# An encoder layer on one core: the last norm's shift is written to the output rows ahead of time, and finished rows are added to it by their stores

## The chip, the cores and the metric

The kernel runs on one core of one Trainium2 chip. The metric is the device time of one execution in microseconds, the median of several runs. PE is the matrix engine, DVE the vector engine, ACT the scalar engine, POOL the GpSimd engine; SP only issues DMAs.

## The reference

One encoder layer (DEPTH is 1) on x of 1024 positions by 1024 channels, in float32: a Fourier token mixer, then a gated MLP with a three-tap convolution over positions, each with a modulated norm ahead of it and a norm behind it. The part that matters here is the end:

```
h = modulate(x, sh2, sc2)
y = conv_gated_ffn(h, *ffn_p[i])                              # F = 2816
x = layer_norm(ALPHA * x + g2[:, None, :] * y, *ln_ffn[i])    # y * g + b per channel
return x
```

The last norm takes mean and variance over the 1024 channels of each position, scales to unit variance, multiplies by a gain per channel (`ffn_g`) and adds a shift per channel (`ffn_b`). Both are given to the kernel as 128 equal rows.

## The kernel before, in words

The work comes in stages: the adaLN vectors and the Fourier mixer (to about 300 us), the up projection with convolution and gate (to about 640 us), the down projection, and the last norm. Matmul operands are split in a high and a low part (ACT copies the high part, DVE or POOL subtracts for the low part, line 54) and each product is three matmuls (`hl3`, lines 284 to 286).

The up projection runs over 22 columns `j` of 128 features. `up_load(j)` issues two loads of 512 KB on SP for each column, and the gated result of each column is stored to `gd` in HBM by a DMA on POOL.

The down projection is a seven-product Strassen scheme over 512 x 512 halves, run in the order of products `(1, 2, 5, 6, 3, 7, 4)`, each over six pairs `i` of blocks; `(p, i)` names a step. `C[half][m]` holds 128 output rows by 1024 channels: half 0 is the upper 512 rows (called u0 to u3 here), half 1 the lower 512 rows (r0 to r3). The upper rows are complete ahead of product 4; `upper_half`, `upper` and `normed` finish them during products 7 and 4: square and sum on ACT (line 877), the power of -0.5 on POOL (line 426, a helper), the small product `nb` on DVE (line 880), the scaling on ACT (line 881), the gain (line 882) and the shift (line 883) on DVE, then `store`, on POOL for the upper half. The lower rows wait for product 4: `lower(m)` prepares them, and `evac(4, m, ...)` multiplies by the gate (line 821 for m of 0 to 2, line 833 in quarters for m of 3), adds (822, 834), takes the variance (827 to 829, or `bn_stats` on lines 835 to 839 for m of 3), takes the power on POOL (830, 840), and then runs two DVE passes over the whole row, line 852 for mean and gain and line 853 for scale and shift, then `store`, on SP for the lower half.

The order of the work on DVE, ACT and PE is chosen by a planner when the kernel is built. From the down projection on, SP and POOL are taken out of that and keep the order in which the program writes their instructions:

```
ctx.enter_context(tc.manual_schedule(engines={mybir.EngineType.SP, mybir.EngineType.Pool}))
```

`ffg` and `ffb` (gain and shift) are loaded on SP at step (7, 1), lines 945 and 947. `E(name)` gives POOL for the names in a fixed list and DVE for the rest; those of the last norm are all DVE.

Of the kernel before, what the change touches and what calls it, by code (L numbers as in the profile page):

```python
# [8 lines left out]
F32 = mybir.dt.float32  # L9
F32R = mybir.dt.float32r  # L10
AF = mybir.ActivationFunctionType
ALU = mybir.AluOpType
# [3 lines left out]
D = 1024  # L16
# [20 lines left out]
def encoder_layer(ctx: ExitStack, tc: tile.TileContext, I, out: bass.AP):  # L37
    nc = tc.nc
    act, dve, pool, pe, sp = nc.scalar, nc.vector, nc.gpsimd, nc.tensor, nc.sync

    cp = ctx.enter_context(tc.tile_pool(name="cp", bufs=1))
    sm = ctx.enter_context(tc.tile_pool(name="sm", bufs=6))
# [3 lines left out]
    def slot(i, shape, dt, name):  # L46
        return big.tile([128] + list(shape), dt, tag=f"s{i}", name=name)
# [8 lines left out]
    def E(name):  # L56
        return pool if name in ON_POOL else dve
# [152 lines left out]
    for t, t4 in pairs:  # L210
# [20 lines left out]
        rs = sm.tile([128, 2], F32, tag="rs2", name=f"rsa{t}")  # L231
# [9 lines left out]
    for c0 in (0, 512):  # L241
        cs = slice(c0, c0 + 512)
# [299 lines left out]
    sp.dma_start(cw, I["cw"])  # L542
    raws = {}

    def up_load(j):
        sl = (24, 27) if j == 0 else ((29, 30) if j % 2 else (27, 28))
        raws[j] = []
        for q in range(2):
            r = slot(sl[q], [4, 256], F32, f"wu{j}_{q}")
            sp.dma_start(r, I["w_up"][j, q])  # L550
            raws[j].append(r)

    up_load(0)
# [70 lines left out]
    A_slots = [33, 34, 35, 45, 46, 47, 48]  # L624
    for j in range(2, NB):
        up_load(j)
        raw = raws[j]
        A11, A21 = raw[0][:, :, 0:128], raw[0][:, :, 128:256]
        A12, A22 = raw[1][:, :, 0:128], raw[1][:, :, 128:256]
        S12 = slot(31, [2, 4, 128], F32, f"S12_{j}")  # L630
        S34 = slot(32, [2, 4, 128], F32, f"S34_{j}")
        S1, S2, S3, S4 = S12[:, 0], S12[:, 1], S34[:, 0], S34[:, 1]
        pool.tensor_tensor(S1, A21, A22, ALU.add)
        pool.tensor_tensor(S2, S1, A11, ALU.subtract)
        pool.tensor_tensor(S3, A11, A21, ALU.subtract)  # L635
        pool.tensor_tensor(S4, A12, S2, ALU.subtract)  # L636

        def product(n, a, tname):
            o = slot(A_slots[n], [2, 4, 128], F32R, f"a{j}_{n}")
            split(o[:, 0], o[:, 1], a)  # L640
            acc = xbank(f"x{j}_{n}")
            th, tl = ops[tname]
            for kt in range(4):
                hl3(acc, o[:, 0, kt, :], o[:, 1, kt, :], th[kt], tl[kt], kt == 0, kt == 3)
            return acc

        if j == NB - 1:
            g2 = slot(27, [D], F32, "g2")
            row_bcast(G2, g2, xbank)
        p12 = slot(6, [2, 512], F32, f"p12_{j}")  # L650
        u34 = slot(7, [2, 512], F32, f"u34_{j}")
        p1, u2, u3, u4 = p12[:, 0], p12[:, 1], u34[:, 0], u34[:, 1]
        uv_ = slot((2 * j) % 3, [S], F32, f"uv{j}")
        ug_ = slot((2 * j + 1) % 3, [S], F32, f"ug{j}")
        x = product(0, A11, "B11")
        act.activation(p1, x, AF.Copy)
        x = product(1, S2, "T2")
        dve.tensor_tensor(u2, x, p1, ALU.add)
        x5 = product(2, S1, "T1")
        dve.tensor_tensor(u4, x5, u2, ALU.add)  # L660
        x = product(3, A12, "B21")
        dve.tensor_tensor(uv_[:, 0:512], x, p1, ALU.add)
        x = product(4, S3, "T3")
        dve.tensor_tensor(u3, x, u2, ALU.add)
        dve.tensor_tensor(ug_[:, 512:], x5, u3, ALU.add)
        x = product(5, S4, "B22")
        dve.tensor_tensor(uv_[:, 512:], x, u4, ALU.add)
        x = product(6, A22, "T4")
        dve.tensor_tensor(ug_[:, 0:512], u3, x, ALU.subtract)
        gated(j, uv_, ug_)  # L670
# [120 lines left out]
        r0 = 512 * half + 128 * m  # L791
        sp.dma_start(xr[half, m], x1d[r0 : r0 + 128, :])

    def store(half, m):
        r0 = 512 * half + 128 * m
        (pool, sp)[half].dma_start(out[r0 : r0 + 128, :], C[half][m])

    def evac(p, m, x):
        c0, c1 = C[0][m], C[1][m]
        nm = f"f{p}{m}"  # L800
        if p == 1:
            act.activation(c1[:, L], x, AF.Copy, scale=-1.0)
        elif p == 2:
            dve.tensor_tensor(c0[:, L], c1[:, L], x, ALU.subtract)
        elif p == 5:
            act.activation(c1[:, R], x, AF.Copy)
        elif p == 6:
            dve.tensor_tensor(c1[:, L], x, c1[:, L], ALU.add)
            dve.tensor_tensor(c1[:, R], c1[:, R], c1[:, L], ALU.add)
        elif p == 3:  # L810
            dve.tensor_tensor(c0[:, R], c1[:, R], x, ALU.subtract)
        elif p == 7:
            dve.tensor_tensor(c1[:, R], c1[:, R], x, ALU.subtract)
            dve.tensor_tensor(c1[:, L], c1[:, L], x, ALU.subtract)
        else:
            st = st1[m]
            t = slot((33, 34)[m % 2], [512], F32, f"pg{m}")
            n = 512 // x_parts(m)
            rs = sm.tile([128, 1], F32, tag="rs", name=f"rs{nm}")
            if m in sq_rows:  # L820
                dve.tensor_tensor(t, x[0], g2[:, L], ALU.mult)
                dve.scalar_tensor_tensor(c1[:, L], t, -1.0, c1[:, L], ALU.mult, ALU.add, accum_out=st[:, 0:1])
                nmu = sm.tile([128, 1], F32, tag="nmu", name=f"nmu{nm}")
                dve.tensor_scalar(nmu, st[:, 0:1], st[:, 1:2], -1.0 / D, ALU.add, ALU.mult)
                ss = sm.tile([128, 1], F32, tag="ss", name=f"ss{nm}")
                junk = cp.tile([128, D], mybir.dt.bfloat16, tag="sel", name=f"junk{nm}")
                act.activation(junk, c1, AF.Square, bias=nmu, accum_out=ss)
                ve = sm.tile([128, 1], F32, tag="ve", name=f"ve{nm}")
                dve.tensor_scalar(ve, ss, 1.0 / D, EPS, ALU.mult, ALU.add)
                pool.tensor_tensor(rs, ve, mhalf, ALU.pow)  # L830
            else:
                for k in range(0, 512, n):
                    dve.tensor_tensor(t[:, k : k + n], x[k // n], g2[:, k : k + n], ALU.mult)
                    dve.tensor_tensor(c1[:, k : k + n], c1[:, k : k + n], t[:, k : k + n], ALU.subtract)
                    dve.bn_stats(st[:, k // n, :], c1[:, k : k + n])
                mv = sm.tile([128, 2], F32, tag="mv", name=f"mv{nm}")
                dve.bn_aggr(mv, st)
                ve = sm.tile([128, 1], F32, tag="ve", name=f"ve{nm}")
                dve.tensor_scalar(ve, mv[:, 1:2], EPS, None, ALU.add)
                pool.tensor_tensor(rs, ve, mhalf, ALU.pow)  # L840
                nmu = sm.tile([128, 1], F32, tag="nmu", name=f"nmu{nm}")
                dve.tensor_scalar(nmu, mv[:, 0:1], -1.0, None, ALU.mult)
            nd = D
            lo, hi = slice(0, nd), slice(nd, D)
            if nd < D:
                nb = sm.tile([128, 1], F32, tag="nb", name=f"nb{nm}")
                E(f"nbt{m}").tensor_tensor(nb, nmu, rs, ALU.mult)
                act.activation(c1[:, hi], c1[:, hi], AF.Identity, scale=rs, bias=nb)
                E(f"ng{m}").tensor_tensor(c1[:, hi], c1[:, hi], ffg[:, hi], ALU.mult)
                E(f"nf{m}").tensor_tensor(c1[:, hi], c1[:, hi], ffb[:, hi], ALU.add)  # L850
            if nd:
                dve.scalar_tensor_tensor(c1[:, lo], c1[:, lo], nmu, ffg[:, lo], ALU.add, ALU.mult)
                dve.scalar_tensor_tensor(c1[:, lo], c1[:, lo], rs, ffb[:, lo], ALU.mult, ALU.add)  # L853
            store(1, m)

    sq_rows = (0, 1, 2)

# [15 lines left out]
    def normed(half, m, nmu):  # L873
        c, nm = C[half][m], f"fn{half}{m}"
        ss = sm.tile([128, 1], F32, tag="ss", name=f"ss{nm}")
        junk = cp.tile([128, D], mybir.dt.bfloat16, tag="sel", name=f"junk{nm}")
        act.activation(junk, c, AF.Square, bias=nmu, accum_out=ss)
        rs = inv_std(ss, nm)
        nb = sm.tile([128, 1], F32, tag="nb", name=f"nb{nm}")
        E(f"unb{m}").tensor_tensor(nb, nmu, rs, ALU.mult)  # L880
        act.activation(c, c, AF.Identity, scale=rs, bias=nb)
        E(f"ug{m}").tensor_tensor(c, c, ffg, ALU.mult)
        E(f"ub{m}").tensor_tensor(c, c, ffb, ALU.add)  # L883
        store(half, m)

    st1 = []
# [28 lines left out]
    for n, (p, i) in enumerate(steps):  # L915
# [27 lines left out]
        if (p, i) == (7, 1):  # L943
            ffg = slot(25, [D], F32, "ffg")
            sp.dma_start(ffg, I["ffn_g"])
            ffb = slot(26, [D], F32, "ffb")
            sp.dma_start(ffb, I["ffn_b"])
        if p == 4 and 0 <= i - 1 < 4:
            lower(i - 1)
        while split_n < min(len(steps), n + 2):  # L950
# [128 lines left out]
```

## Time and profile before

| | |
|---|---|
| runs, median | 871.85 us (869.87 to 873.02, 3 runs) |
| profiled execution, time | 872.16 us |
| profiled execution, span | 870.4 us |
| granted PE clock, mean | 0.974 |
| PE busy | 798.9 us (92%) |
| DVE busy | 720.4 us (83%) |
| ACT busy | 387.8 us (45%) |
| POOL busy | 312.9 us (36%) |
| DMA moved | 131.02 MB, mean 151 GB/s |

The span runs from the first to the last event of the profiled execution; the time has some 1.8 us around it. Busy shares are averages over all stages, so the rows of one stretch say more than this table. In rows of a timeline the columns are the start in us from the span's start, the duration in us, the engine, the line, the operation and its output and inputs. A bracket at the end says how long the engine was idle before, and what released it. An instruction's duration on DVE and ACT takes in some pipeline time, so that the next one can start a little before it ends.

### The profile page before, as it was taken

To read this page: it belongs to the slowest core of one execution; us is meant where nothing else is said; L and a number is where in the kernel's file an instruction comes from. 1 tells how busy PE (TensorE), PEld (TensorE's weight loads), DVE (VectorE), ACT (ScalarE), POOL (GpSimd) and SP (SyncE) were. 2 spreads that over 40 slices of the span, in tenths; PEclk is the share of its full clock that TensorE was granted. 3 is DMA by queue.
4 is the path that set the end of the run, shared out by engine and by line. 5 is a ranking of instruction groups with operands and counts; after the bars stand their busy time and mean duration, and the time that the engine had idled before them with its cause. 6 is when DMAs were issued, how large, how long until landed. Compare 5 with 4: busy or idle time off the path is not lost.

```text
span 870.4 us, 10731 instructions
## 1 busy us (share of the span) xinstructions
PE 798.9 (92%) x3943; PEld 644.0 (74%) x3943; DVE 720.4 (83%) x991; ACT 387.8 (45%) x559; POOL 312.9 (36%) x244
## 2 busy tenths in 40 slices
PE   2699799998979999999999999999999989999990
PEld 1466577877858888888888888888878868887880
DVE  6972857899899999998888888888677795556998
ACT  7442514577454344444444444444454324335612
POOL 4776802498355444334343333431000122301102
PEclk9899899999989999999999999999999999999995
DMA  9658665572112212322212222210598886808703
GB/s 344 252 183 306 248 228 198 178 270 81 49 49 97 98 73 76 116 85 88 73 72 73 98 97 81 89 49 25 186 375 296 279 213 113 157 25 270 261 27 143
DMA packets 49749, 131.02 MB, mean 151 GB/s; under 512 B 5512, under 2 KB 6664, under 8 KB 49696
## 3 DMA queue, kind: packets, MB, share of 16 engines
q1 hardware_dynamic: 41008, 106.47, 34.6%
q0 software_dynamic: 8400, 22.81, 9.8%
q10 hardware_dynamic: 288, 1.05, 0.3%
q8 instruction: 31, 0.51, 0.2%
q14 instruction: 22, 0.18, 0.1%
HBM read 110.39 MB, written 19.92 MB: 150 GB/s over the span
## 4 chain that ended last, share of the span: by engine, by line
PE 54%; DVE 8%; DMA 7%; issue 3%; POOL 1%; SPq 0%; ACT 0%; DVEq 0%; POOLq 0%
PE x L286 14%; PE x L284 14%; PE x L285 14%; PE o L285 4%; PE o L286 4%; PE o L284 4%; DMA gr<-gd 2%; DMA xu<-x1d 2%; DVE d_1l L54 2%; DMA wd<-in_w_down_dram 1%; DVE d_0l L54 1%; DMA wd_2r<-in_w_down_dram 1%; DMA Sg<-gd 1%; DVE C L853 1%; DVE C L883 1%
## 5 line engine op out<-in xcount | busy, mean ns | idle before, releaser
L284 PE MATMUL x<-Hh,a 128*128 128x512 f32 (+2 forms) x416 | 155.8, 378 | 5.3 <-ACT a L53 5.3
L285 PE MATMUL x<-Hl,a 128*128 128x512 f32 (+2 forms) x416 | 156.6, 377 | 3.9 <-DVE Hl L54 3.1
L286 PE MATMUL x<-Hh,a 128*128 128x512 f32 (+2 forms) x416 | 155.8, 375 | 0.0
L285 PE MATMUL o<-d_1l,d_0h 128*128 128x512 f32 (+1 forms) x299 | 115.0, 385 | 6.5 <-DVE d_1l L54 4.3
L286 PE MATMUL o<-d_1h,d_0l 128*128 128x512 f32 (+1 forms) x299 | 114.7, 384 | 0.0
L284 PE MATMUL o<-d_1h,d_0h 128*128 128x512 f32 (+1 forms) x299 | 102.4, 382 | 0.0
L284 PEld LDWEIGHTS x<-Hh,a 128*128 128x128 f32 x416 | 78.7, 191 | 21.2 <-ACT a L53 6.0
L285 PEld LDWEIGHTS x<-Hl,a 128*128 128x128 f32 x416 | 79.0, 190 | 19.2 <-DVE Hl L54 4.4
L53 ACT ACTIVATE a<-S 128x512 fp32r<-128x512 f32 x80 | 50.4, 630 | 95.6 <-PE x L286 87.2
L286 PEld LDWEIGHTS x<-Hh,a 128*128 128x128 f32 x416 | 78.9, 190 | 14.5 <-issue 0.8
L588 POOL DMA_DIRECT2D gd<-ug x20 | 11.4, 569 | 170.2 <-DVE ug L587 170.2
L285 PEld LDWEIGHTS o<-d_1l,d_0h 128*128 128x128 f32 x299 | 56.6, 189 | 18.7 <-DVE d_1l L54 7.7
L54 DVE TENSOR_TENSOR a<-wu,a 128x512 fp32r<-128x512 f32 x60 | 63.6, 1060 | 3.0 <-ACT a L53 3.0
L286 PEld LDWEIGHTS o<-d_1h,d_0l 128*128 128x128 f32 x299 | 56.6, 189 | 10.8
L284 PEld LDWEIGHTS o<-d_1h,d_0h 128*128 128x128 f32 x299 | 56.3, 189 | 11.0
L54 DVE TENSOR_TENSOR a<-S,a 128x512 fp32r<-128x512 f32 x80 | 61.0, 763 | 0.8
L53 ACT ACTIVATE a<-wu 128x512 fp32r<-128x512 f32 x60 | 37.5, 625 | 40.1 <-PE x L286 38.2
L635 POOL TENSOR_TENSOR S<-wu 128x512 f32<-128x512 f32 x20 | 29.8, 1492 | 69.0 <-DVE a L54 60.3
L735 POOL DMA_DIRECT2D Sg<-gd x12 | 13.9, 1239 | 91.6 <-DVE d_0l L54 91.6
L579 DVE SCALAR_TENSOR_TENSOR t<-uv,cw,t 128x1023 f32<-128x1023 f32 x20 | 35.9, 1793 | 11.4 <-ACT t L578 11.3
L636 POOL TENSOR_TENSOR S<-wu,S 128x512 f32<-128x512 f32 x20 | 43.9, 2195 | 0.1
L53 ACT ACTIVATE d_0h<-Sg 128x1024 fp32r<-128x1024 f32 x15 | 15.9, 1062 | 58.1 <-PE o L285 58.1
(341 smaller groups left out, 1944.5 us busy)
## 6 DMA issues: line engine op xcount, KB each, us to landing
aw<-in_ada_w_dram SPq DMA_DIRECT2D x48, 512.0 KB, 6.2
wu<-in_w_up_dram SPq DMA_DIRECT2D x44, 512.0 KB, 3.2
gd<-ug POOLq DMA_DIRECT2D x20, 512.0 KB, 2.9
wd<-in_w_down_dram SPq DMA_DIRECT2D x20, 512.0 KB, 9.7
gr<-gd SPq DMA_DIRECT2D x15, 512.0 KB, 7.6
gA<-gd SPq DMA_DIRECT2D x10, 512.0 KB, 10.7
Sg<-gd POOLq DMA_DIRECT2D x10, 512.0 KB, 6.2
x<-in_x_dram SPq DMA_DIRECT2D x8, 512.0 KB, 6.1
```

Source lines behind the costliest of these rows:

```text
L53: act.activation(hi, src, AF.Copy)
L54: (eng or dve).tensor_tensor(lo, src, hi, ALU.subtract)
L284: pe.matmul(ps_ap, hi_l, hi_r, start=first, stop=False)
L285: pe.matmul(ps_ap, hi_l, lo_r, start=False, stop=False)
L286: pe.matmul(ps_ap, lo_l, hi_r, start=False, stop=last)
L579: dve.scalar_tensor_tensor(tt[:, 1:S], u[:, 0 : S - 1], w[:, 0:1], tt[:, 1:S], ALU.mult, ALU.add)
L588: pool.dma_start(gd[j], gg)
L635: pool.tensor_tensor(S3, A11, A21, ALU.subtract)
L636: pool.tensor_tensor(S4, A12, S2, ALU.subtract)
L735: pool.dma_start(raw_g[p, i] if p == 7 else Sg[i], gd[k0 : k0 + n, :, 512 * mh : 512 * mh + 512].rearrange("k p c -> p k c"), accum_op=ALU ...
L853: dve.scalar_tensor_tensor(c1[:, lo], c1[:, lo], rs, ffb[:, lo], ALU.mult, ALU.add)
L883: E(f"ub{m}").tensor_tensor(c, c, ffb, ALU.add)
```

## The change

During the up projection, each of the columns 4 to 11 issues one more DMA on SP: a copy of the 128 shift rows (`ffn_b`, 512 KB) from HBM straight to 128 rows of the output in HBM, placed behind that column's weight loads. After eight columns the whole output holds the shift. The later stores no longer overwrite: they add to what is there (`accum_op=ALU.add`), which DMAs issued from POOL can do, so all stores go out on POOL. The shift is no longer loaded to SBUF, and no engine adds it.

For the upper rows the DVE add of line 883 goes. For the lower rows, the two DVE passes of lines 852 and 853 become: a small product `nb` on DVE, the scaling on ACT, the product with the gain on DVE. The last row (m of 3) does scaling, product and store in two halves of 512 channels, the right half first.

```diff
+    up_load_ins = []
...
-            sp.dma_start(r, I["w_up"][j, q])
+            up_load_ins.append(sp.dma_start(r, I["w_up"][j, q]))
...
     for j in range(2, NB):
         up_load(j)
+
+        if 4 <= j < 12:
+            with tc.issue_after(up_load_ins[-1].ins):
+                sp.dma_start(out[128 * (j - 4) : 128 * (j - 3), :], I["ffn_b"])
...
-    def store(half, m):
+    def store(half, m, cs=slice(0, D)):
         r0 = 512 * half + 128 * m
-        (pool, sp)[half].dma_start(out[r0 : r0 + 128, :], C[half][m])
+        pool.dma_start(out[r0 : r0 + 128, cs], C[half][m][:, cs], accum_op=ALU.add)
...
-            nd = D
-            lo, hi = slice(0, nd), slice(nd, D)
...
-            if nd:
-                dve.scalar_tensor_tensor(c1[:, lo], c1[:, lo], nmu, ffg[:, lo], ALU.add, ALU.mult)
-                dve.scalar_tensor_tensor(c1[:, lo], c1[:, lo], rs, ffb[:, lo], ALU.mult, ALU.add)
-            store(1, m)
+            nb = sm.tile([128, 1], F32, tag="nb", name=f"nb{nm}")
+            dve.tensor_tensor(nb, nmu, rs, ALU.mult)
+            for hs in (R, L) if m == 3 else (slice(0, D),):
+                act.activation(c1[:, hs], c1[:, hs], AF.Identity, scale=rs, bias=nb)
+                dve.tensor_tensor(c1[:, hs], c1[:, hs], ffg[:, hs], ALU.mult)
+                store(1, m, hs)
...
-        E(f"ub{m}").tensor_tensor(c, c, ffb, ALU.add)
         store(half, m)
...
-            ffb = slot(26, [D], F32, "ffb")
-            sp.dma_start(ffb, I["ffn_b"])
```

`tc.issue_after(x)` only places the block's DMA behind `x` in SP's order; it waits for nothing.

More of the change, by code (lines that the diff above doesn't have):

```diff
@@ L842, in evac @@
                 dve.tensor_scalar(nmu, mv[:, 0:1], -1.0, None, ALU.mult)
-            nd = D
-            lo, hi = slice(0, nd), slice(nd, D)
[L845 to L850, printed above, removed]
-            if nd:
-                dve.scalar_tensor_tensor(c1[:, lo], c1[:, lo], nmu, ffg[:, lo], ALU.add, ALU.mult)
-                dve.scalar_tensor_tensor(c1[:, lo], c1[:, lo], rs, ffb[:, lo], ALU.mult, ALU.add)
-            store(1, m)
+            nb = sm.tile([128, 1], F32, tag="nb", name=f"nb{nm}")
[4 more added lines that the diff above has]
+                store(1, m, hs)
     sq_rows = (0, 1, 2)
```

## Prediction

> **What bounds the end now.** I read the busy time by stretch first, then the end of DVE, ACT and POOL in order of time, then the transfers.
>
> ```profile
> core 0: us, PE busy (x) PEld busy (x) DVE busy (x) ACT busy (x) POOL busy (x), PEclk, DMA share, GB/s
> 300.00:660.00 360.00, 359.54 (x1587) 297.46 (x1586) 315.18 (x391) 158.56 (x207) 113.78 (x83) 1.00 0.30 109
> ...
> 826.70:846.00 19.30, 19.30 (x107) 16.78 (x106) 19.30 (x35) 2.40 (x3) 0.56 (x1) 1.00 0.07 28
> 846.00:848.30 2.30, 2.23 (x19) 2.03 (x17) 2.30 (x4) 0.00 (x0) 0.88 (x2) 1.00 0.00 0
> 848.30:867.00 18.70, 0.00 (x0) 0.00 (x0) 17.99 (x35) 4.86 (x7) 5.00 (x6) 0.61 0.35 141
> ```
>
> PE is the bound through the up projection and still full to 848.3; then 18.7 us follow without a matmul, with DVE busy 17.99 of them. The change works on this end. Rows u0 to u3 below are the upper half of the output, r0 to r3 the lower half.
>
> ```profile
> 809.61 1.22 DVE L883 TENSOR_TENSOR C<-C,ffb 128x1024 f32<-128x1024 f32 x1
> 824.49 1.22 DVE L883 TENSOR_TENSOR C<-C,ffb 128x1024 f32<-128x1024 f32 x1
> 845.89 1.21 DVE L883 TENSOR_TENSOR C<-C,ffb 128x1024 f32<-128x1024 f32 x1
> 847.03 1.27 DVE L821 TENSOR_TENSOR pg<-o,g 128x512 f32<-128x512 f32 x2
> 848.88 0.67 DVE L822 SCALAR_TENSOR_TENSOR C<-pg,C 128x512 f32<-128x512 f32 x1
> 850.10 0.14 DVE L880 TENSOR_TENSOR nbfn<-nmufu,rs_fn 128x1 f32<-128x1 f32 x1
> 850.17 0.20 DVE L824 TENSOR_SCALAR nmuf<-stl 128x1 f32<-128x1 f32 x1
> 850.34 1.24 ACT L881 ACTIVATE C<-C,nbfn,rs_fn 128x1024 f32<-128x1024 f32 x1 [15.10 <-DVE nbfn L880]
> 851.48 1.13 ACT L827 ACTIVATE junkf<-C,nmuf 128x1024 bf16<-128x1024 f32 x1
> 852.52 0.19 ACT L827 ACTIVATION_READ_ACCUMULATOR junkf<-C,nmuf 128x1 f32 x1
> 852.62 1.21 DVE L882 TENSOR_TENSOR C<-C,ffg 128x1024 f32<-128x1024 f32 x1
> 854.21 0.13 DVE L829 TENSOR_SCALAR vef<-ssf 128x1 f32<-128x1 f32 x1
> 857.05 1.21 DVE L883 TENSOR_TENSOR C<-C,ffb 128x1024 f32<-128x1024 f32 x1
> 864.02 1.28 DVE L852 SCALAR_TENSOR_TENSOR C<-C,nmuf,ffg 128x1024 f32<-128x1024 f32 x1
> 865.40 1.28 DVE L853 SCALAR_TENSOR_TENSOR C<-C,rsf,ffb 128x1024 f32<-128x1024 f32 x1
> ```
>
> The reader sees DVE finishing u2 (845.89), closing r0 to r3 (from 847.03), finishing u3 in the holes (852.62, 857.05) and ending with the two full passes of each lower row. POOL matters as much:
>
> ```profile
> 822.16 0.14 DVE L424 TENSOR_SCALAR ve_fn<-ssfn 128x1 f32<-128x1 f32 x1
> ...
> 847.40 0.58 POOL L796 DMA_DIRECT2D out_dram<-C  x1 [20.14 <-DVE C L883]
> 848.00 0.57 POOL L426 TENSOR_TENSOR rs_fn<-ve_fn,mhalf 128x1 f32<-128x1 f32 x1
> 858.55 0.57 POOL L796 DMA_DIRECT2D out_dram<-C  x1 [9.98 <-DVE C L883]
> 859.14 2.85 POOL L830 TENSOR_TENSOR rsf<-vef,mhalf 128x1 f32<-128x1 f32 x3
> 861.97 1.34 POOL L840 TENSOR_TENSOR rsf<-vef,mhalf 128x1 f32<-128x1 f32 x1
> ...
> L796 SPq DMA_DIRECT2D out_dram<-C x4: 332/334/338, 861.6 to 866.7; - x4
> ...
> out_dram<-C SPq DMA_DIRECT2D x4, 512.0 KB, 2.6
> ```
>
> u3's power had its input at 822.3 and ran at 848.00, right behind u2's store; r0's had its input at 854.34 and ran at 859.14, right behind u3's store. So POOL keeps the written order, and a store that waits for its row holds every power behind it. The last store goes out on SP at 866.7 and lands 2.6 later, at 869.3; 1.1 more to the span's end, 870.4. The profiled execution took 872.16 around that span, the median shown is 871.85. I work on the span and put the difference onto the median.
>
> **The change, part by part.**
>
> Removed: four L883 adds. One holds DVE for 1.14 (845.89 to 847.03). Two of them (809.61, 824.49) lie in a stretch where DVE never pauses, so what follows comes 2.27 earlier; the third is the one before 847.03 itself. Together r0 could start at 847.03 - 3.4 = 843.6, but its product must be there:
>
> ```profile
> 844.29 0.40 PE L286 MATMUL o<-d_1h,d_0l 128*128 128x512 f32 x1
> ...
> 847.96 0.28 PE L286 MATMUL o<-d_1h,d_0l 128*128 128x256 f32 x1
> ```
>
> The first row is the last product of r0 (three 512-wide blocks close one after the other, then r3's 256-wide ones), ending 844.7; the second ends PE at 848.24. PE was full, so these stay. r0 starts at 844.9: 2.1 gained, not 3.4. If DVE is held up elsewhere the gain is zero.
>
> Moved: the lower rows' two DVE passes, L852 and L853 (1.28 each), become one ACT pass like L881 (1.24), one DVE product like L882 (1.21) and a tiny nb like L880 (0.14). DVE gets shorter by 4 x 1.2 us; ACT stood almost idle. But the stores go from SP to POOL, and there they stand between the powers: in written order POOL now has store u3, power r0, store r0, power r1, store r1, and so on. Where three powers ran together at 859.14, power r1 must now wait until r0 is scaled, multiplied and handed to its store. This is the price of the change: one closed round per row. Its steps, from the rows above: power 0.57; to DVE 0.2; nb 0.14; to ACT 0.1 (850.24 to 850.34); scaling 1.24; to DVE 0.05; product 1.21; to POOL 0.30 (847.10 to 847.40); store 0.58. That is 4.39 a row, 13.2 for three rows.
>
> Start of the first round: it needs store u3 gone and r0's variance. u2's product stays, its add goes, so store u2, power u3 and u3's nb all come some 5 us earlier (L882 of u3 then has the hole in which L883 of u2 stood, or one soon after). r0's variance: 844.9 + 3.07 (847.03 to 850.10: L821 and L822 of r0 and r1) + 0.2 (L824) + 1.33 (the square and its sum, 851.48 to 852.71, and a start) + 0.13 = 849.6 with nothing between. With u3's product between, 1.14 later, 850.8. I take 850.8, because L882 of u3 fell among these instructions before. Lower end 849.6.
>
> The last row is split in halves. Its power starts at 850.8 + 13.2 = 864.0, nb is through at 865.0. Halves of this size have rows:
>
> ```profile
> 833.15 0.62 ACT L53 ACTIVATE d_1h<-wd_10r 128x512 fp32r<-128x512 f32 x1
> 838.10 0.68 DVE L891 TENSOR_TENSOR C<-C,g 128x512 f32<-128x512 f32 x1
> ```
>
> 865.0 + 0.62 + 0.05 + 0.68 + 0.30 = 866.7 for the first half's store; 0.58 later, 867.3, the second's, whose product (ACT to 866.3, DVE to 867.0) is just done.
>
> The adding stores have no row of their own; these are nearest:
>
> ```profile
> q0 software_dynamic: 1389, 2.68, 101.2%
> ...
> L735 POOL DMA_DIRECT2D Sg<-gd x12: 1188/1197/1422, 684.3 to 745.0; - x12
> DMA to landing us min/median/max: 5.4/6.8/14.8
> ...
> out_dram<-C POOLq DMA_DIRECT2D x2, 512.0 KB, 2.9
> ```
>
> The first is the stretch 745 to 760, in which adding transfers alone filled all 16 engines: 2.68 MB in 15 us, 0.18 MB per us, so 1.4 us of data for a 256 KB half; a plain store of 512 KB took 2.9 in all. An adding transfer of 512 KB took at least 5.4, but with 1.2 of issue against 0.58 here. So the last half lands between 2.9 and 5.4 after its issue; I take 3.5, since half the bytes at half the speed resembles the plain whole row, plus some queueing behind the first half. 867.3 + 3.5 + 1.1 = 871.9. Against 870.4 that is 1.5 more: 871.85 + 1.5 = 873.35.
>
> The Trainium skill, "DMA: Bandwidth & Descriptors" (Anatomy of one DMA), puts a POOL-issued transfer at about 2.0 us plus its bytes over 436 GB/s. By it the last half would land in an estimated 2.6, and the sum would be 872.4; it holds for the plain store's 2.9, not for the 5.4 of the adding ones.
>
> Added: eight copies of 512 KB from HBM to HBM on SP, one behind each of eight weight loads.
>
> ```profile
> wu<-in_w_up_dram SPq DMA_DIRECT2D x44, 512.0 KB, 3.2
> ...
> 792.28 1.06 SPq L947 DMA_DIRECT2D ffb<-in_ffn_b_dram  x1
> ...
> DVE wd_0r L746 <- DMA wd_0r<-in_w_down_dram: 3.1, 1, 3.1
> ```
>
> A copy costs SP 0.33 and the queues between 1.3 and 2.8 us (plain store to adding speed). A weight pair lands 3.2 after its issue and has a column of about 360/22 = 16 us; DMA is 0.30 busy there. I cost them at nothing; without this cover, 8 x 2.8 = 22. The L947 load (512 KB, 1.06 of SP) goes from a crowded stretch, but the wait there, 3.1 for wd_0r, is for a load issued ahead of it: between 0 and 1 gained, I take 0. The adding stores of u0 to u2 double their transfer time in a stretch where DVE and PE read operands loaded long before: 0.
>
> **The rivals.**
>
> u3 holds the queue. If DVE's order leaves L882 of u3 where it is (852.62, less 2.1: 850.5), store u3 goes out at 852.0, power r0 at 852.6: 875.1. If it slides to where L883 stands (857.05 less 2.1 and 1.1), power r0 starts at 855.9: 878.4. For it: u2 and u3 were finished last in every hole, and power u3 waited 26 us. Against: its input comes 5 us earlier. It decides from a power r0 later than 852.0. About 876; chance 0.26.
>
> Row 0 first. If L821 and L822 of r0 run back to back, power r0 starts at 847.8, 3.0 earlier; with rounds of 4.07 (DVE and ACT free at once, as instructions follow each other at 1.14) another 1.0 goes: 869.3, and with the plain landing 2.9, 868.7. For it: DVE has room. Against: before, r0 and r1 went in pairs. Chance 0.14.
>
> The powers run ahead of the stores. Then DVE would bound: its end at 866.7 less 2.1 (r0's start), less 1.14 (u3's add) and 4 x 1.2 (one pass of each lower row), 858.7; with the store's 0.9, 3.5 and 1.1 the span would be 864.2, the time 865.7. The rows at 848.00 and 859.14 speak against it. Chance 0.05.
>
> Slow powers. The power took 0.57 at 848.00, 0.95 in the group at 859.14, 1.34 at 861.97, the slow ones beside DVE passes with two SBUF inputs (L852, L853). If all four ran at 0.95, 1.5 more: 874.85. In the closed round DVE has nothing to run beside a power, save for r0's. Chance 0.05. The Trainium skill, "SBUF — State Buffer" (Who interferes with whom), says just this: a DVE instruction with two SBUF inputs contends with a GpSimd one that reads SBUF. The three durations agree with it.
>
> The copies stall the weights: up to 22 more, 894; PE's 359.54 of 360 shows no such wait today. Chance 0.03.
>
> **How the numbers follow.** Some 2.6 us (0.3%) is what can be told from no change. The closed round has 0.47 and lies within it at 873.35, its own range 871 to 874.5. Slower: late u3, slow powers, copies, 0.34. Faster: row 0 first and powers ahead, 0.19. The range from 868.7 to 877 leaves out the powers ahead, the copies and part of the late u3.
>
> **What would show it.** On POOL each power of r1 to r3 right behind the store of the row before, 4.4 us apart; no L883; r0's first pass at about 845; a power r0 near 850.8; the last landing 3.5 after its issue; PE's share of 300 to 660 unchanged. I am wrong if powers stand together, if power r0 comes after 852, or if a weight load ends a PE wait during the up projection.

## The result and the profile after

The changed kernel takes 876.07 us (median; 874.93 to 879.71), the one before 871.74 in the same session: a ratio of 1.0054, 95% interval 1.0039 to 1.0068. It is slower by 4.3 us (4.7 by the ratio), clear of the noise, where 1.5 had been forecast, which could not have been told from no change. The profiled execution took 875.91 around a span of 874.1.

The stretch of the up projection, the same columns as before:

```profile
300.00:660.00 360.00, 360.00 (x1591) 298.07 (x1590) 316.18 (x389) 159.07 (x209) 113.75 (x83) 1.00 0.33 119
```

The copies are there (DMA share 0.33 for 0.30, 119 GB/s for 109) and PE is as full as before. So the difference lies in the end. The last matmul, and POOL behind it:

```profile
846.03 0.28 PE L286 MATMUL o<-d_1h,d_0l 128*128 128x256 f32 x1
...
843.01 0.87 POOL L802 DMA_DIRECT2D out_dram<-C  x1 [14.66 <-DVE C L882]
848.39 0.66 POOL L836 TENSOR_TENSOR rsf<-vef,mhalf 128x1 f32<-128x1 f32 x1 [4.51 <-DVE vef L835]
852.78 0.88 POOL L802 DMA_DIRECT2D out_dram<-C  x1 [3.73 <-DVE C L853]
853.39 0.86 POOL L836 TENSOR_TENSOR rsf<-vef,mhalf 128x1 f32<-128x1 f32 x1
857.27 0.87 POOL L802 DMA_DIRECT2D out_dram<-C  x1 [3.02 <-DVE C L853]
857.88 0.85 POOL L836 TENSOR_TENSOR rsf<-vef,mhalf 128x1 f32<-128x1 f32 x1
861.81 0.88 POOL L802 DMA_DIRECT2D out_dram<-C  x1 [3.08 <-DVE C L853]
862.41 0.86 POOL L846 TENSOR_TENSOR rsf<-vef,mhalf 128x1 f32<-128x1 f32 x1
865.34 1.76 POOL L802 DMA_DIRECT2D out_dram<-C  x2 [2.06 <-DVE C L853]
```

Where three powers stood in one group before, each power of r1 to r3 now follows the store of the row before it, and each of those stores comes after 3 us and more of idle time on POOL, which ended with that row's product (L853). The powers start 5.00, 4.49 and 4.53 apart. One round on DVE and ACT, between the stores at 852.78 and 857.27:

```profile
854.28 0.16 DVE L850 TENSOR_TENSOR nbf<-nmuf,rsf 128x1 f32<-128x1 f32 x1 [1.80 <-POOL rsf L836]
854.48 1.24 ACT L852 ACTIVATE C<-C,nbf,rsf 128x1024 f32<-128x1024 f32 x1 [3.26 <-DVE nbf L850]
855.75 1.23 DVE L853 TENSOR_TENSOR C<-C,ffg 128x1024 f32<-128x1024 f32 x1 [1.31 <-ACT C L852]
```

DVE, which had hardly a pause before (17.99 of 18.7 us busy), now waits for POOL and for ACT in turn. Then the close. The rows are groups of a line's instructions with smallest, median and largest duration in ns, then first and last start; the line is the program's end:

```profile
L1072 POOLq DRAIN  x3: 40/102/7341, 866.0 to 873.9; - x3
L1072 SPq DRAIN  x3: 7/7/7, 871.5 to 873.6; - x3
...
out_dram<-C POOLq DMA_DIRECT2D x2, 256.0 KB, 4.5
```

and the same two groups of the kernel before:

```profile
L1075 POOLq DRAIN  x3: 40/93/5312, 861.8 to 870.1; - x3
L1075 SPq DRAIN  x3: 7/7/7, 869.6 to 869.9; - x3
```

A DRAIN is the instruction with which an engine's queue closes at the end of the program. SP reaches its closing DRAIN when the last transfer has landed. Before, that was 869.6, and POOL's long DRAIN had been over since 861.8 + 5.3 = 867.1. Now SP is there at 871.5, but POOL's DRAIN lasts from 866.0 to 873.3, and the program ends behind it. The last half store was issued at 866.0 and landed 5.3 later, at 871.3, which is 0.2 ahead of SP's first DRAIN (before: 869.3, 0.3 ahead).

### The profile page after: what moved, and what is told of

The parts are those of the page before. It is cut to its first block, busy times and chain, and to the rows that moved or that the text cites. A ratio compares the mean times of both kernels' runs of the same rounds, so it can differ in the third digit from the quotient of the medians.

```text
span 874.1 us, 10747 instructions
## 1 busy us (share of the span) xinstructions
PE 797.4 (91%) x3943; PEld 642.0 (73%) x3943; DVE 712.8 (82%) x988; ACT 392.3 (45%) x564; POOL 318.0 (36%) x249
## 4 chain that ended last, share of the span: by engine, by line
PE 58%; DVE 5%; DMA 5%; issue 3%; POOL 1%; ACT 1%; SPq 0%; POOLq 0%; DVEq 0%; ACTq 0%
PE x L284 14%; PE x L285 14%; PE x L286 14%; PE o L285 5%; PE o L286 5%; PE o L284 5%; DMA xu<-x1d 2%; DMA wd_2r<-in_w_down_dram 1%; DMA gA<-gd 1%; DVE d_0l L54 1%; DVE d_1l L54 1%; DMA Sg<-gd 1%; POOL S L641 0%; DVE C L853 0%; ACT C L852 0%
## 5 line engine op out<-in xcount | busy, mean ns | idle before, releaser
L581 DVE SCALAR_TENSOR_TENSOR t<-uv,cw,t 128x1023 f32<-128x1023 f32 x20 | 35.9, 1793 | 11.4 <-ACT t L580 11.2
## 6 DMA issues: line engine op xcount, KB each, us to landing
gA<-gd SPq DMA_DIRECT2D x10, 512.0 KB, 11.2
```

Source lines behind the costliest of these rows:

```text
L581: dve.scalar_tensor_tensor(tt[:, 1:S], u[:, 0 : S - 1], w[:, 0:1], tt[:, 1:S], ALU.mult, ALU.add)
```

## The experiments

PE's last matmul starts between 846.0 and 850.5 in the profiles of this study, which scatter in the stages ahead of the end. So besides the time I give the tail, from the start of PE's last matmul to the end of the span: 870.4 - 847.96 = 22.4 before, 874.1 - 846.03 = 28.1 changed. The tail comes from one profile of each kernel (two of the changed one), and it does not always agree with the time to better than 2 us. The ratios are against the kernel before, run in the same session.

| kernel | time, us | ratio (95%) | tail, us |
|---|---|---|---|
| before | 871.74 | 1 | 22.4 |
| changed | 876.07 | 1.0054 (1.0039 to 1.0068) | 28.1 |
| changed, second session | 878.14 | 1.0062 (1.0043 to 1.0081) | 28.4 |
| copies alone | 871.79 | 1.0002 (0.9987 to 1.0018) | 22.4 |
| upper rows alone | 868.65 | 0.9966 (0.9953 to 0.9980) | 17.5 |
| powers first | 873.22 | 1.0017 (1.0005 to 1.0029) | 23.1 |
| powers first, plain stores on POOL | 868.06 | 0.9944 (0.9931 to 0.9958) | 17.1 |
| lower stores plain on SP | 864.75 | 0.9926 (0.9906 to 0.9946) | 14.2 |
| last row plain on SP | 874.45 | 1.0024 (1.0011 to 1.0037) | 23.5 |
| before, last store on POOL | 874.33 | 1.0027 (1.0012 to 1.0043) | 24.7 |
| mixed | 867.94 | 0.9943 (0.9931 to 0.9956) | 17.4 |
| mixed, r1 on DVE | 867.78 | 0.9940 (0.9922 to 0.9958) | 16.7 |

Three kernels (powers first with plain stores on POOL, lower stores plain on SP, last row plain on SP) put plain stores in place of adding ones and leave the shift out of those rows. They measure a cost and are no versions to use.

The theory: closed rounds on POOL, one per lower row. The rivals: the adding transfers and their completion, whatever the order; and the copies.

**Powers first.** `nb`, scaling, product and store of the lower rows move into a function that is called once all four powers are written.

```diff
+        for f in fins:        # behind the loop over m
+            finish(*f)        # nb, act.activation, dve.tensor_tensor, store
```

> The changed kernel with one thing altered: on POOL the four powers of the lower rows are written ahead of their stores, so no power waits for a store. Closed-round theory (the end is set by power, scaling, product and store of one row running before the next row's power): the three rounds of 4.7 us fall away, the rows follow one another at ACT's 1.24 us, the last product ends near 856; then the four adding stores (2.1 MB at the 0.18 MB per us of adding transfers, 11.5 us) bind, landing near 865, with 2.8 us to the end a span near 868 and a time of about 870. Rival (the adding transfers and their completion set the loss, not the order): the time stays within 2 us of the changed kernel's 876.

873.22 us, between the 870 of the theory and the 874 to 878 of the rival. The powers stand together and the stores follow:

```profile
850.25 0.66 POOL L836 TENSOR_TENSOR rsf<-vef,mhalf 128x1 f32<-128x1 f32 x1 [4.51 <-DVE vef L835]
851.09 0.55 POOL L836 TENSOR_TENSOR rsf<-vef,mhalf 128x1 f32<-128x1 f32 x1 [0.17 <-DVE vef L835]
852.22 0.55 POOL L836 TENSOR_TENSOR rsf<-vef,mhalf 128x1 f32<-128x1 f32 x1 [0.59 <-DVE vef L845]
852.73 0.55 POOL L846 TENSOR_TENSOR rsf<-vef,mhalf 128x1 f32<-128x1 f32 x1
854.64 0.88 POOL L802 DMA_DIRECT2D out_dram<-C  x1 [1.36 <-DVE nbf L856]
855.85 0.85 POOL L802 DMA_DIRECT2D out_dram<-C  x1 [0.33 <-DVE C L859]
856.98 2.62 POOL L802 DMA_DIRECT2D out_dram<-C  x3 [0.28 <-DVE C L859]
...
L1081 POOLq DRAIN  x3: 40/93/11983, 858.2 to 870.6; - x3
L1081 SPq DRAIN  x3: 7/7/7, 868.3 to 870.4; - x3
```

All stores are out by 859.6, against 867.1 in the changed kernel, but SP is released only at 868.3: 8.7 us later, where 4.4 passed in the changed kernel. Counted from PE's last matmul the stores are out at 11.8 instead of 21.1. So the rounds were real; but behind them stood a second limit, the adding transfers, and of the 9.3 us only 5.0 reach the end of the span. The theory was right about the rounds and not about their weight.

**The lower rows' stores plain and on SP.**

```diff
-        pool.dma_start(out[r0 : r0 + 128, cs], C[half][m][:, cs], accum_op=ALU.add)
+        # lower rows:
+        sp.dma_start(out[r0 : r0 + 128, cs], C[half][m][:, cs])
```

> The changed kernel with the lower rows' stores plain and on SP (it leaves the shift out of the lower rows). No store stands between the powers and no adding transfer at the end: both theories expect the rows to follow at ACT's 1.24 us, the last product near 856, a landing 2.6 later and 1.1 to the end: span near 860, time about 862. The distance from this to the kernel with the powers first is the price of the adding transfers and their end; its distance to the changed kernel is the whole price of the stores, 14 us. If it stays above 868, neither theory holds and ACT or DVE binds.

864.75 us, where 862 had been forecast; the tail is 14.2, and PE's last matmul started 2.6 later in this profile than in that of the kernel before. The last product ended 10.0 us behind PE's last matmul, as in the kernel with the powers first; what differs between these two is the stores alone, 8.9 us of tail.

**Powers first, stores on POOL but plain**, on top of the powers-first kernel:

```diff
-        pool.dma_start(out[r0 : r0 + 128, cs], C[half][m][:, cs], accum_op=ALU.add)
+        # lower rows:
+        pool.dma_start(out[r0 : r0 + 128, cs], C[half][m][:, cs])
```

> The kernel with the powers first, its lower rows' stores still on POOL but plain (it leaves the shift out of the lower rows). It splits the distance between the powers-first kernel (873.2) and the one with SP stores (864.8) into adding and POOL. If the doubled transfer time of the adding stores makes the distance: about 867 (POOL's issue and its closing wait stay, 2.5 us over the SP kernel). If POOL's issue and closing wait make it, adding or not: 871 or more.

868.06 us, near the 867 that goes with the doubled transfer time. The adding is worth 23.1 - 17.1 = 6.0 of the tail, POOL in place of SP 17.1 - 14.2 = 2.9. The software queue's groups, in a window from 853 to just past the span's end, show the adding; columns are packets, MB and the share of 16 engines, then the issues with the median us to landing. Plain stores (15 us):

```profile
q0 software_dynamic: 592, 2.10, 36.0%
...
out_dram<-C POOLq DMA_DIRECT2D x3, 512.0 KB, 3.3
out_dram<-C POOLq DMA_DIRECT2D x2, 256.0 KB, 3.8
```

and adding stores, with the powers first (18 us):

```profile
q0 software_dynamic: 720, 2.10, 65.2%
...
out_dram<-C POOLq DMA_DIRECT2D x3, 512.0 KB, 7.2
out_dram<-C POOLq DMA_DIRECT2D x2, 256.0 KB, 9.5
```

The same 2.10 MB held the engines for 0.360 x 15 x 16 = 86 engine-us and for 0.652 x 18 x 16 = 188: more than twice.

**The copies alone**, in the kernel before, with its plain stores writing over them:

```diff
+        if 4 <= j < 12:
+            with tc.issue_after(up_load_ins[-1].ins):
+                sp.dma_start(out[128 * (j - 4) : 128 * (j - 3), :], I["ffn_b"])
```

> The kernel before with the eight copies added and nothing else; the plain stores overwrite them. Closed-round theory: hidden, 871.7 within 1 us, and no PE wait for a weight load in the up projection. Rival (the copies disturb the weight loads or the gated stores): 2 to 4 us more than before, most of the change's loss.

871.79 us, ratio 1.0002, and PE busy 359.48 of 360 us in the up projection. That rival of 2 to 4 us falls; the interval leaves room for 1.6 at most.

**The upper rows alone.**

```diff
+        if 4 <= j < 8:        # four copies, in up_load's loop
...
-        (pool, sp)[half].dma_start(out[r0 : r0 + 128, :], C[half][m])
+        # upper: pool.dma_start(..., accum_op=ALU.add); lower: sp.dma_start(...)
...
-        E(f"ub{m}").tensor_tensor(c, c, ffb, ALU.add)
```

> The kernel before with the change made for the upper rows alone: four copies during the up projection, adding stores for u0 to u3, no L883; the lower rows keep their two DVE passes, ffb in SBUF and plain stores on SP. Closed-round theory: the loss lies in the lower rows alone, so this keeps the 3.7 us earlier start of the lower rows and loses two DVE passes from the end: last pass near 861, span near 865, time about 866.5, faster than before by 5. Rival (the copies or the adding stores cost time by themselves): 872 to 876.

868.65 us: 3.0 faster than before, not 5, but clear. The tail is 4.9 shorter, near the forecast 5; but PE's last matmul started 1.3 later in this profile, and whether that is scatter or belongs to the change was not settled. In this half of the change the adding stores go out while PE still works, so neither their landing nor POOL's closing is at the end.

**The last row's two stores plain and on SP**, the rest as changed:

```diff
+        if (half, m) == (1, 3):
+            sp.dma_start(out[r0 : r0 + 128, cs], C[half][m][:, cs])
```

> The changed kernel with only the last row's two half stores plain and on SP (it leaves the shift out of that row); the closed rounds stay. Theory (the last landing of 5.2 and the 2.8 behind it cost 3.5 to 4.5 us against an SP store): about 871.7 to 872.5. Rival (the rounds are all that counts and the end is as long with an SP store): 875 to 876.

874.45 us, a ratio 0.0030 lower than the changed kernel's (2.6 us), a tail 4.6 shorter. The time lies above the 871.7 to 872.5 of the theory and just under the 875 to 876 of the rival; only the tail shows the gain that the theory gave (3.5 to 4.5). The rounds are still there, and the close is shorter, though r2's adding store still holds it:

```profile
L1075 POOLq DRAIN  x3: 40/93/7465, 864.1 to 872.1; - x3
L1075 SPq DRAIN  x3: 7/7/7, 871.3 to 871.8; - x3
```

POOL's long DRAIN ends at 864.1 + 7.5 = 871.6, 0.3 behind SP's first.

**The kernel before with its last store on POOL**, plain:

```diff
-        (pool, sp)[half].dma_start(out[r0 : r0 + 128, :], C[half][m])
+        (sp if half and m < 3 else pool).dma_start(out[r0 : r0 + 128, :], C[half][m])
```

> The kernel before with the store of its last row issued on POOL in place of SP, plain as it was. Theory (POOL's own closing wait after a late POOL-issued transfer is part of the loss): POOL's issue and landing cost 0.5 more than SP's, and the end comes 2.8 us after the landing, as in the changed kernel, not 1.1: about 874. Rival (the long end belongs to adding transfers): 872.3.

874.33 us; the theory's number. The rows are the store, then the two closing groups:

```profile
866.70 0.57 POOL L796 DMA_DIRECT2D out_dram<-C  x1 [3.67 <-DVE C L853]
...
L1075 POOLq DRAIN  x3: 40/102/4873, 866.7 to 872.1; - x3
L1075 SPq DRAIN  x3: 7/7/7, 870.1 to 871.8; - x3
```

The store was issued at the same place as on SP before (866.7) and took a little longer to land; the end then waited for POOL's DRAIN, over at 866.7 + 4.9 = 871.6, when SP, with the last landing at 869.6, was ready at 870.1. One changed engine for one plain store of 512 KB costs 0.27%.

**The changed kernel again**, without an edit.

> The changed kernel as it is, for a second profile. In its first profile PE ended at 846.0, 1.9 us earlier than before, and the tail from there was 28.1. If the earlier PE end is scatter between executions, this profile has PE's last matmul anywhere from 846 to 850 with a tail of 28.1 again; if it comes from the change, near 846 again. Powers of r1 to r3 again right behind the stores, 4.5 apart. Time 875 to 877.

878.14 us, above the 875 to 877 that was expected. PE's last matmul is at 848.8 and the tail is 28.4, with the powers 4.99, 4.49 and 4.54 apart. So the early 846.0 of the first profile was scatter.

**Two mixed versions**, meant to keep the gains: powers first, upper rows and r0 by adding stores, r1 to r3 with the shift from SBUF and plain stores on SP.

```diff
+            if m > 0:
+                (pool if m == 1 else dve).tensor_tensor(c1[:, hs], c1[:, hs], ffb[:, hs], ALU.add)
```

> A version meant to keep the gains: powers first; the upper rows and r0 by adding stores (five copies); r1's shift added on POOL, which is idle then, r2's and r3's on DVE; their stores plain on SP. Theory: DVE does six passes after the powers instead of four, the last store goes out some 12 to 13 us after PE's end against 10.6 in the kernel with four SP stores, no adding transfer is late: 866 to 867.5, better than the 868.7 of the kernel with the upper rows alone. Rival (POOL's add of a whole row, 2.9 us, and its reads beside DVE's passes hold DVE or r1's store): 868.5 or more.

> The mixed version with r1's shift on DVE in place of POOL, so that POOL does no whole-row pass. In the mixed version POOL's pass took 3.24 us, and three DVE products beside it took 5.10 in place of 3.5. Theory (shared reads of POOL and DVE cost those 1.6 us): DVE does seven passes of 1.14 back to back, the last store goes out 1 us earlier, time about 867. Rival (r1's add on DVE costs the 1.14 that POOL took over and nothing comes back): 868 to 868.5.

867.94 and 867.78 us. Both are faster than the kernel before by 0.6%; the times do not tell them from each other. The first came out between its theory (866 to 867.5) and its rival (868.5 or more), and the second missed its 867 and came near its rival's 868. In the first, POOL's pass holds up DVE:

```profile
856.32 3.24 POOL L864 TENSOR_TENSOR C<-C,ffb 128x1024 f32<-128x1024 f32 x1
...
L862 DVE TENSOR_TENSOR C<-C,ffg x5: 677/1219/2828, 853.8 to 861.2; 128x1024 f32<-128x1024 f32 x3, 128x512 f32<-128x512 f32 x2
```

One of the two half-row products took 2.83 us, the other 0.68: it began at 857.27, while POOL's pass was under way, and ended 0.5 behind it. The whole-row product that had started ahead of POOL's pass kept its 1.22. In the second version the half row in question is back to its pace:

```profile
859.11 0.68 DVE L862 TENSOR_TENSOR C<-C,ffg 128x512 f32<-128x512 f32 x1
```

So 2.15 us came back for 1.14 of added work; of the difference of 1.0 the tail shows 0.7 (16.7 for 17.4).

## Why the prediction was right and wrong

**The number.** In part it came out by luck. Counted from PE's last matmul the end was forecast 4.2 too short, as added up below, and the time only 2.7: in the profiled execution, whose time is near the median, PE ended 1.9 early, which the repeat shows to be scatter. The median of the repeat, 878.14, lies above the stated 868.7 to 877.

**The engine and the place.** Right: the loss is in the end, the copies are hidden, PE's share in the up projection is the same.

**r0 starts 2.1 earlier.** Nearly. Counted from PE's last matmul, r0's first pass (L821, now L827 at 843.29) stood 0.9 ahead of it before and stands 2.7 ahead now: 1.8.

**Power r0 at 850.8.** Earlier than that: 848.39, 2.4 behind PE's last matmul where 2.8 was forecast. Store u3 was out at 843.01, and the power waited for r0's own variance. So the rival of a late u3, to which I gave the largest chance after the forecast, did not happen. That the offset came near was luck in part: the forecast put u3's product between r0's steps, and it ran ahead of all of them. In its place r0's variance was held on DVE, behind passes of other rows, from 847.2, when ACT had the sum of squares, to 848.15:

```profile
841.50 1.22 DVE L882 TENSOR_TENSOR C<-C,ffg 128x1024 f32<-128x1024 f32 x1
...
847.00 0.19 ACT L833 ACTIVATION_READ_ACCUMULATOR junkf<-C,nmuf 128x1 f32 x1
848.15 0.14 DVE L835 TENSOR_SCALAR vef<-ssf 128x1 f32<-128x1 f32 x1
```

**Rounds of 4.39, three of them 13.2.** Right in kind and size: 14.0, because the first took 5.00. In it, ACT was still at the third row's square until 850.0, and r0's scaling waited for it. The powers took 0.85, not 0.57, but began while the store ahead of them was still shown as running.

**Halves.** From power r3 to the second half's store 3.6, forecast 3.3.

**The last landing, 3.5.** Too small: 5.3. The bounds given (2.9 to 5.4) held it; I took a value near the plain store, reasoning that half the bytes at half the speed are a plain row. For the first half, the one issue in the view from 861.8 to 866 of this size, that was nearly so:

```profile
out_dram<-C POOLq DMA_DIRECT2D x1, 256.0 KB, 3.8
```

The second was issued 0.7 behind it and took 5.3. That fits queueing behind the first half, whose data are an estimated 1.4 us (256 KB at the 0.18 MB per us of adding transfers), and 3.5 left almost no room for it; no run here stores one half alone. By the Trainium skill, "DMA: Bandwidth & Descriptors" (Anatomy of one DMA), it would have been an estimated 2.6; for the plain 512 KB store's 2.9 its sum is an estimated 3.2. Both adding halves took longer, and so did the plain halves on POOL (3.8 at the median), which came last of five stores in a row.

**1.1 from landing to the end.** This step failed. I carried it over from a store on SP to one on POOL without a bound. It was 2.8: POOL's DRAIN ended 2.0 after the last landing of a POOL transfer, in the changed kernel (871.3 to 873.3) and in the kernel before with its last store on POOL (869.6 to 871.6). With the powers first and plain stores on POOL it was 2.1 (860.2 + 3.8 = 864.0 to 866.1), so this does not come from the adding.

The landing is not all that the DRAIN's end goes by. In the kernel before, POOL's last transfer had landed at 858.55 + 2.9 = 861.5, and the DRAIN still ended at 867.1, hidden under the SP stores: 3.8 after POOL's last power (863.3). With the lower rows' stores on SP it also ended 3.8 after the last power (855.96 to 859.73). So a late operation on POOL can hold the end by itself. If a store's issue counts like a power, that alone would have ended the DRAIN of the kernel before with its last store on POOL at an estimated 867.3 + 3.8 = 871.1, against the 871.6 that it had, so this run by itself hardly tells the two apart. In the changed kernel the same sum gives 867.1 + 3.8 = 870.9 against 873.3, and there the landing decided.

From PE's last matmul the forecast's tail was 871.9 - 847.96 = 23.9. The measured 28.1 is 4.2 longer: -0.5 for power r0, +0.8 for the rounds, +0.3 for the halves, +1.8 for the landing, +1.7 for the close, 4.1 together and the rest rounding. The close was carried over without a bound, and the landing is as large a miss inside its bounds.

**Slow powers** beside DVE passes with two SBUF inputs: the lower rows of the upper-rows-alone kernel show powers of 1.5 to 1.6 us beside such passes, and the powers-first kernel 0.55 beside small ones. This agrees with the Trainium skill, "SBUF — State Buffer" (Who interferes with whom), by which a DVE instruction with two SBUF inputs contends with a GpSimd one that reads SBUF. In the changed kernel DVE was idle beside the powers of r1 to r3 and ran small passes beside r0's (0.66), so this cost it nothing that could be told.

**What the loss is made of**, as the runs take it apart. With the powers first and the stores plain on SP, the end's tail is 14.2, 8.2 shorter than before; that is what the removed DVE passes are worth by this measure (6.5 by the ratio). The stores take back 2.9 for being on POOL, 6.0 for adding and 5.0 for standing between the powers, 13.9 together. The first two are measured with the rounds gone; with the rounds in place the adding transfers are spread out and part of their price is hidden in the rounds. The ratios give the same order, with 1.6, 6.4 and 3.2 us, 11.2 together. The intervals of the two plain kernels overlap, so the price of POOL in place of SP rests on the tails and on the one moved store (0.27%). Why the rounds come to 5.0 by the tails and 3.2 by the ratios (3.9 with the second session's) was not settled.

## What to carry to other kernels

An operation moved onto a queue that keeps its written order has to be costed with everything written behind it: here a cheap store became a gate between rows, and writing all the small powers ahead of all the stores brought the last store forward by 9.3 us, of which some 3 to 5 reached the end. A step that is free in the middle of a kernel can cost its full latency at the end: adding stores in place of DVE's adds gained 3 us for the rows finished while PE still ran, and lost more than that for the rows finished last. For the last transfer of a program, count the landing, what stands ahead of it in its queue, and the issuing engine's own closing, and take none of them from a transfer on another engine.

## What the hardware showed that I had not expected

- An adding store of SBUF rows to HBM held the transfer engines for more than twice the time of a plain one (188 engine-us for 86, 2.10 MB each).
- The program's end waited for POOL's DRAIN, which ended some 2.0 us after the last POOL-issued transfer had landed, where that came last, whether it added (871.3 to 873.3) or not (864.0 to 866.1, powers first with plain stores). Where the transfers had landed long before, the DRAIN still ended 3.8 us after POOL's last operation (863.3 to 867.1).
- A half-row product on DVE that began during a whole-row add on POOL (3.24 us) took 2.83 us in place of 0.68.
